# Layer 1's modulation sums placed in the gate and up phase, and more raw slabs in flight in the context's down pass

## The chip, the cores and the metric

The kernel runs on one core of a Trainium2 chip. The metric is the device time of one execution in microseconds (us), and the median of several runs counts. Five engines work side by side, each on its own instructions in a fixed order: TensorE (PE, matrix products), VectorE (DVE, element-wise work), ScalarE (ACT, activations and copies), GpSimd (POOL) and SyncE (SP), which here issues nearly all transfers between HBM and the on-chip memory, one after the other from a single queue.

## The reference, cut to what matters

The model has two layers over 1024 latent tokens (`x`) and 256 context tokens (`ctx`), 1024 channels wide. Each layer scales and shifts its normed input by modulation vectors, sends it through three token mixers and an output projection, and then through a gated feed-forward block of 2816 hidden channels:

```python
for l in range(2):
    mod = silu_c @ w_ada[l] + b_ada[l]              # six vectors of 1024: the modulation
    sh_a, sc_a, g_a, sh_f, sc_f, g_f = split(mod)
    mc = split(silu_cc @ w_ada[l][:, :n_c] + ...)    # the same for the context; 2 vectors in layer 1
    hx = rmsnorm(x) * (1 + sc_a) + sh_a
    ...                                              # Fourier mixing, attention, gated recurrence
    x = x + g_a * (concat(fx, ax, rx) @ w_out[l])
    x = x + g_f * swiglu(rmsnorm(x) * (1 + sc_f) + sh_f, w_gate[l], w_up[l], w_down[l])
    if l == 0:                                       # the context takes the same path in layer 0 only
        ctx = ctx + mc[2] * (concat(fc, ac, rc) @ w_out[l])
        ctx = ctx + mc[5] * swiglu(rmsnorm(ctx) * (1 + mc[4]) + mc[3], ...)
return rmsnorm(x, final_norm)
# swiglu(h) = (silu(h @ w_gate) * (h @ w_up)) @ w_down, all of it in float32
```

## The kernel before

**Exact products out of rounded ones.** Each float32 operand is split into a rounded high part and the rest. `split` (line 123) makes the high part on ACT (line 124, a cast) and the low part on DVE (line 125, a subtraction). `mm3` (line 127) then issues three matmuls: high weight by high activation (L131), high weight by low activation (L132) and low weight by high activation (L133). In tile names `hw` and `lw` are the parts of weights, `mh` and `ml` (or `a`, `T`) those of activations. Weights come from HBM as float32 into raw slots (tag `raw`, RAWB=2 of them) and are split into pairs of slots (tags `wh` and `wl`, WB=4 each). So a raw slot is free again when DVE has done its subtraction, and a pair when PE has used it.

**Tokens in three chunks.** Chunk 0 is the context (256 columns), chunks 1 and 2 are the latent tokens (512 columns each). In layer 0 all three are computed, in layer 1 the feed-forward part has only the latent tokens.

**The operand stage (`operands`, line 1041).** Between the output projection (blocks `oacc`, called as `block(d, ci)`) and the first gate product, the residual rows are normed and modulated. `norm(ci)` adds squares over channels with a ones matmul (`ss`, L403) and takes the root. `rows` modulates one block of 128 channels, and `put` splits it into an operand pair. The latent chunks are multiplied by a fast scheme for 2 by 2 blocks, with seven products named "11", "21", "T1", "T2", "22", "T3" and "T4"; sums and differences of the operand rows (`T`, lines 1092 to 1112) are formed first. The differences for "T3" run on POOL (L1105).

**Gate and up (`fast_product` line 1142, `ffn` line 1243).** For each of 11 column groups g, the gate weight and then the up weight go through the seven products: 84 matmuls of 512 columns, and in layer 0 another 48 of 256 columns for the context (`fpc`). DVE mixes weights (`wm`, L1162), makes their low parts, and combines the products (L1188). The gated result leaves for HBM (`da`, L1136).

**The down passes (`down_pass` line 1251, `down_next` line 1290).** In layer 0 the chunks are taken in the order 1, 2, 0, each with the whole of `w_down`: the results of gate and up are read back (`ar`, L1260) and split into `a`; then for each pair (or four) of output blocks, slabs of 128x512 weights are loaded (`rwd`, L421 in `slab`), split and multiplied into `fd`. A pass has 48 slabs. After each slab, `step` is called once.

**What `step` does.** In chunks 1 and 2 it advances layer 1's modulation sums (`ada_sums`, line 248) by one piece. These read the whole of layer 1's `w_ada` in 96 loads of 128x512 (`wa`, 256 KB each, WAB=2 slots), each multiplied by a scalar per partition and added into a sum `as` on DVE (L278, or L280 for the first of a group; 128 operations in all). A group of four sums (tag `acc`, ACB=4 slots) is then reduced over partitions by ones matmuls (`adas`, L286), copied (`adar`), transposed (`adat`, L301) and put into `mod`. In chunk 0, `step` instead modulates the new rows of chunks 1 and 2 for layer 1's mixers (L324 to L331, with half of the low parts on POOL, L328).

**Who sets the order.** The program is written once in Python; a scheduler with a timing model of its own orders each engine's instructions when the program is built. On the chip each engine keeps that order and waits on semaphores. SP holds the transfers of all these stages in one order too, so a transfer that waits for its slot holds up those behind it.

Of the kernel before, what the change touches and what calls it, by code (L numbers as in the profile page):

```python
# [10 lines left out]
F32 = mybir.dt.float32  # L11
# [72 lines left out]
ACB = 4  # L84
# [15 lines left out]
class Kern:  # L100
# [147 lines left out]
    def ada_sums(self, l, blocks, tags):  # L248
# [5 lines left out]
        groups = [blocks[i:i + 4] for i in range(0, len(blocks), 4)]  # L254
# [39 lines left out]
    def ada_columns(self, l, ps, group):  # L294
# [3 lines left out]
        nc.scalar.copy(out=rowsb, in_=ps)  # L298
        pt = self.ps("pv", f"adat{l}")
        for b in range(4):  # L300
            nc.tensor.transpose(pt[:, b * P:(b + 1) * P], rowsb[:, b * P:(b + 1) * P], self.c["ident"])  # L301
# [115 lines left out]
    def slab(self, src, name, halves=False):  # L417

        nk = src.shape[1]
        raw = self.wp.tile([P, nk, P], F32, tag="raw", name="r" + name, bufs=RAWB)  # L420
# [145 lines left out]
    def unit_prepare(self, l, i, j, ci, ops):  # L566
# [38 lines left out]
        mh = self.sp.tile([8, 2, P], F32R, tag="mh", name="mh", bufs=2)  # L605
# [434 lines left out]
    def operands(self, l, slab, block, ss):  # L1040
# [21 lines left out]
        for d in range(4, KD):  # L1062
            slab(d)
            if l == 0:
                block(d, 0)
            block(d, 1)
        slab(4)
        if l == 0:
            rc = self.rstd(self.square_sum(ss[0], 0), CTX, D, f"f{l}rc", "pa", PAB)
        norm(1)  # L1070
        u = []
        for d in range(4, KD):
# [3 lines left out]
            for e in (2 * d - 8, 2 * d - 7):  # L1076
                u.append(rows(e, 1))
                put(("11", "21")[e // 4], u[e], self.hh[e][:, c1], self.hl[e][:, c1])
                if l == 0:
                    self.modulate(self.xT[e][:, 0:CTX], rc[:, :CTX], e, 1, l, 4, 3, self.hh[e][:, 0:CTX], self.hl[e][:, 0:CTX])  # L1080
        puts = self.puts(0)
        self.fp = itertools.cycle(("mm", "sc", "mx", "pv"))
        first = [self.fast_product(l, w, 0, *tb, put, True) for w, tb, put in zip(("w_gate", "w_up"), (("pa", PAB), ("t2", TB)), puts)]
        next(first[0])
        norm(2)
# [15 lines left out]
        for k in range(4):  # L1101
            put("22", v[4 + k], self.hh[4 + k][:, c2], self.hl[4 + k][:, c2])
# [37 lines left out]
    def fast_product(self, l, w, g, tag, bufs, put, early=False):  # L1140
# [53 lines left out]
        c = context_block()  # L1194
        context(c, a, 0, True)
# [3 lines left out]
        context(c, a, 1, False)  # L1199
# [10 lines left out]
        if l == 0:  # L1210
            put(0, 0, c)
# [24 lines left out]
        if l == 0:  # L1236
            c = context_block()
            context(c, a, 1, True)
            context(c, operand(A[1][0]), 0, False)
            put(1, 0, c)  # L1240

    def ffn(self, l):
        for g in range(1, NFF // 2):
            gate, up = self.puts(g)
            for _ in self.fast_product(l, "w_gate", g, "pa", PAB, gate):
                pass
            for _ in self.fast_product(l, "w_up", g, "t2", TB, up):
                pass
# [3 lines left out]
    def down_pass(self, l, ci, groups, tags, take, step=lambda: None):  # L1252
# [4 lines left out]
        rooms = []  # L1257
        for f in range(NFF):
# [262 lines left out]
```

## Time and profile before

| | before |
|---|---|
| median of 3 runs | 3312.84 us (3311.32 to 3314.97) |
| the profiled execution | 3315.27 us |
| its span in the trace | 3313.5 us |
| mean granted TensorE clock | 0.98 of full speed |
| PE busy | 3170.5 us, 96% |
| DVE busy | 1977.4 us, 60% |
| ACT busy | 1394.4 us, 42% |
| POOL busy | 104.5 us, 3% |
| read from HBM | 282.00 MB |

Busy time of PE is modelled: a matmul's end is worked out, so PE can look busy while its matmuls follow each other at less than full speed. The distance between the starts of consecutive matmuls tells more. The program falls into stages one after the other: layer 0's mixers and output projection (to about 900 us), its operand stage (about 875 to 976), gate and up (to 1476), the down passes for chunks 1, 2 and 0 (1476 to 1879), then layer 1's mixers (to about 2600), its operand stage, gate and up (to 3046) and its two down passes (to 3301).

### The profile page before, as it was taken

What the parts mean: (1) busy time and instruction counts of PE and PEld (TensorE: products, weight loads), DVE (VectorE), ACT (ScalarE), POOL (GpSimd) and SP (SyncE); (2) the same over time, 40 slices, a digit from 0 to 9 for tenths busy, and PEclk for the clock granted to TensorE, in tenths of its full rate; (3) what the DMA queues carried; (4) which work ended last, traced back from release to release, by engine and by line L of the source; (5) the groups of instructions that cost most, each with busy time, mean ns of one, the idle gap of its engine ahead of it and who ended that gap; (6) DMA issues with size and microseconds to landing.
All of it is one profiled execution on the core that took longest, in us unless ns stands there. A gap on an engine that the chain in (4) does not pass through costs nothing.

```text
span 3313.5 us, 44692 instructions
## 1 busy us (share of the span) xinstructions
PE 3170.5 (96%) x16810; PEld 2335.8 (70%) x16810; DVE 1977.4 (60%) x3463; ACT 1394.4 (42%) x2526; POOL 104.5 (3%) x77
## 2 busy tenths in 40 slices
PE   7999999999989999998997899999999899999998
PEld 4977544456868888886776788645556578887887
DVE  5298767552575555566756336677633766667343
ACT  5255455453442322333424334454463533334343
POOL 1000000000110000000001000000000100000000
PEclk9999999999999999998998999999999899999999
DMA  8346110035312122147875432201034222224453
GB/s 275 114 147 218 40 64 29 20 94 176 101 52 71 62 75 71 63 155 230 253 211 172 123 123 81 90 19 62 27 96 159 73 84 85 89 81 159 149 172 95
DMA packets 358657, 369.50 MB, mean 112 GB/s; under 512 B 21896, under 2 KB 268072, under 8 KB 358440
## 3 DMA queue, kind: packets, MB, share of 16 engines
q1 hardware_dynamic: 358440, 366.65, 35.2%
q8 instruction: 131, 2.15, 0.3%
q14 instruction: 86, 0.70, 0.1%
HBM read 282.00 MB, written 84.41 MB: 111 GB/s over the span
## 4 chain that ended last, share of the span: by engine, by line
PE 79%; DMA 8%; DVE 7%; ACT 3%; issue 2%; POOL 0%; SPq 0%; ACTq 0%; DVEq 0%; POOLq 0%
PE fp L131 8%; PE fp L132 8%; PE fp L133 8%; PE pv L639 6%; PE fd L133 3%; PE fd L131 3%; PE fd L132 3%; PE mx L596 3%; DMA rwd<-in_w_down_dram 3%; PE sm L644 3%; PE sc L630 3%; PE u L131 3%; PE u L132 3%; PE u L133 3%; PE sc L631 2%; DMA wa<-in_w_ada_dram 2%
## 5 line engine op out<-in xcount | busy, mean ns | idle before, releaser
L131 PE MATMUL fd<-a,hwd 128*128 128x512 f32 (+1 forms) x880 | 338.0, 384 | 34.3 <-ACT hwd L124 34.3
L133 PE MATMUL fd<-a,lwd 128*128 128x512 f32 (+1 forms) x880 | 337.6, 384 | 17.6 <-DVE lwd L125 17.3
L132 PE MATMUL fd<-a,hwd 128*128 128x512 f32 (+1 forms) x880 | 333.9, 379 | 0.1
L597 DVE TENSOR_REDUCE mp<-mx 128x1 f32<-128x512 f32 (+1 forms) x400 | 223.9, 591 | 131.4 <-PE mx L596 129.9
L125 DVE TENSOR_TENSOR lwd<-rwd,hwd 128x512 fp32r<-128x512 f32 (+1 forms) x240 | 157.3, 657 | 223.2 <-ACT hwd L124 207.6
L124 ACT CAST hwd<-rwd 128x512 fp32r<-128x512 f32 (+1 forms) x240 | 140.1, 584 | 354.6 <-DMA rwd<-in_w_down_dram 196.8
L633 ACT ACTIVATE p<-sc 128x512 f32<-128x512 f32 (+1 forms) x336 | 185.9, 586 | 185.6 <-PE sc L631 182.8
L639 PE MATMUL pv<-p,V 128*64 128x512 f32 (+1 forms) x672 | 230.6, 607 | 0.0
L131 PEld LDWEIGHTS fd<-a,hwd 128*128 128x128 f32 x880 | 174.0, 198 | 70.8 <-ACT hwd L124 40.6
L133 PEld LDWEIGHTS fd<-a,lwd 128*128 128x128 f32 x880 | 173.8, 198 | 55.5 <-DVE lwd L125 27.7
L132 PEld LDWEIGHTS fd<-a,hwd 128*128 128x128 f32 x880 | 173.9, 198 | 30.2 <-issue 1.9
L278 DVE SCALAR_TENSOR_TENSOR as<-wa,sc,as 128x512 f32<-128x512 f32 x224 | 161.2, 748 | 47.4 <-DMA wa<-in_w_ada_dram 46.5
L131 PE MATMUL fp<-mh,hw_gate 128*128 128x512 f32 x352 | 140.3, 399 | 7.7 <-ACT hw_gate L124 4.0
L133 PE MATMUL fp<-mh,lw_gate 128*128 128x512 f32 x352 | 139.5, 396 | 4.4 <-DVE lw_gate L125 4.4
L132 PE MATMUL fp<-ml,hw_gate 128*128 128x512 f32 x352 | 140.0, 398 | 1.6 <-DVE ml L1059 1.5
L131 PE MATMUL fp<-mh,hw_up 128*128 128x512 f32 x352 | 138.4, 393 | 0.2 <-ACT hw_up L124 0.2
L132 PE MATMUL fp<-ml,hw_up 128*128 128x512 f32 x352 | 137.5, 391 | 0.0
L133 PE MATMUL fp<-mh,lw_up 128*128 128x512 f32 x352 | 137.2, 390 | 0.1
L131 PE MATMUL u<-a0hh,hwin 128*128 128x512 f32 (+1 forms) x360 | 133.2, 372 | 3.4 <-ACT a0hh L330 2.1
L132 PE MATMUL u<-a0hl,hwin 128*128 128x512 f32 (+1 forms) x360 | 129.6, 362 | 3.9 <-POOL a0hl L328 2.4
L131 PE MATMUL oacc<-mh,hwo 128*128 128x512 f32 (+1 forms) x320 | 122.2, 384 | 9.8 <-ACT mh L124 8.4
L133 PE MATMUL u<-a0hh,lwin 128*128 128x512 f32 (+1 forms) x360 | 127.8, 356 | 0.0
(356 smaller groups left out, 7398.7 us busy)
## 6 DMA issues: line engine op xcount, KB each, us to landing
rwd<-in_w_down_dram SPq DMA_DIRECT2D x200, 256.0 KB
wa<-in_w_ada_dram SPq DMA_DIRECT2D x192, 256.0 KB
rw_gate<-in_w_gate_dram SPq DMA_DIRECT2D x44, 512.0 KB
rw_up<-in_w_up_dram SPq DMA_DIRECT2D x44, 512.0 KB
da<-mw_gate SPq DMA_DIRECT2D x88, 256.0 KB
ar<-da SPq DMA_DIRECT2D x88, 256.0 KB
rwin<-in_w_in_dram SPq DMA_DIRECT2D x30, 512.0 KB
rwo<-in_w_out_dram SPq DMA_DIRECT2D x24, 512.0 KB
```

The costliest lines, as they stand in the source:

```text
L124: self.nc.scalar.copy(out=hi, in_=src)
L125: self.nc.vector.tensor_tensor(out=lo, in0=src, in1=hi, op=ALU.subtract)
L131: self.nc.tensor.matmul(out, lh, rh, start=(first and i == 0), stop=False)
L132: self.nc.tensor.matmul(out, lh, rl, start=False, stop=False)
L133: self.nc.tensor.matmul(out, ll, rh, start=False, stop=(last and i == n - 1))
L278: nc.vector.scalar_tensor_tensor(out=acc, in0=w, scalar=sc, in1=acc, op0=ALU.mult, op1=ALU.add)
L596: nc.tensor.matmul(mx[:, :kn], Q1[a][:, t * P:(t + 1) * P], self.K1[g][:, k0:k0 + kn])
L597: nc.vector.tensor_reduce(out=mp[:, a * nt + t, i:i + 1], in_=mx[:, :kn], axis=AX.X, op=ALU.max)
L630: nc.tensor.matmul(sc[:, :n], self.K1[g][:, ks], Q1[a], start=True, stop=False)
L633: nc.scalar.activation(out=pf, in_=sc[:, :n], func=AF.Exp, scale=0.125)
L639: nc.tensor.matmul(pv[64 * a:64 * a + 64, :n], self.V[:, i, 64 * g:64 * g + 64], ps[i][a], start=(i == 0), stop=(i == nk - 1))
L644: nc.tensor.matmul(sm[r:r + 32, :n], self.c["first"], ps[i - 1 + o][a], start=(i == 1), stop=(i == nk - 1), tile_position=(0, r))
```

## The change

1. Layer 1's sums move from the steps of the down passes for chunks 1 and 2 into `ffn`: each of the five yields of every gate and up product for g = 1 to 10 advances them by one piece; what is left is issued ahead of the down passes. They are taken in eight groups of two sums instead of four groups of four. `ada_columns` copies and transposes only the rows that are used.
2. In the context's down pass the raw slabs cycle through one slot of tag `raw` and two of tag `acc`; ACB is 5 instead of 4, so that 2 + 5 raw slabs can be in flight. In the other passes the raw slabs use the two raw slots as before.
3. In the operand stage, `norm(2)` is issued ahead of the first products. In layer 0 two of the context's output blocks, (6, 0) and (7, 0), follow it, and the context's norm and modulation come after the operands of "T4". The first products of gate and up (g = 0) do their context part at their end; for this two more weight blocks per product are split again.
4. The low parts of operand "22" are subtracted on POOL instead of DVE, in both layers.
5. The slots for the softmax's row maxima (`mh`) go from two to one.

```diff
-ACB = 4
+ACB = 5
...
-    def ada_sums(self, l, blocks, tags):
+    def ada_sums(self, l, blocks, tags, size=4):
...
-        groups = [blocks[i:i + 4] for i in range(0, len(blocks), 4)]
+        groups = [blocks[i:i + size] for i in range(0, len(blocks), size)]
...
-        nc.scalar.copy(out=rowsb, in_=ps)
+        n = 32 * (max(r for r, g in group) // 32 + 1)
+        nc.scalar.copy(out=rowsb[0:n], in_=ps[0:n])
...
-            nc.tensor.transpose(pt[:, b * P:(b + 1) * P], rowsb[:, b * P:(b + 1) * P], self.c["ident"])
+            nc.tensor.transpose(pt[:, b * P:b * P + n], rowsb[0:n, b * P:(b + 1) * P], self.c["ident"][0:n, 0:n])
...
-        raw = self.wp.tile([P, nk, P], F32, tag="raw", name="r" + name, bufs=RAWB)
+        raw = (self.wp if tag[0] == "raw" else self.tp).tile([P, nk, P], F32, tag=tag[0], name="r" + name, bufs=tag[1])
...
-        mh = self.sp.tile([8, 2, P], F32R, tag="mh", name="mh", bufs=2)
+        mh = self.sp.tile([8, 2, P], F32R, tag="mh", name="mh", bufs=1)
...
-            if l == 0:
+            if l == 0 and d < KD - 2:
                 block(d, 0)
...
-        if l == 0:
-            rc = self.rstd(self.square_sum(ss[0], 0), CTX, D, f"f{l}rc", "pa", PAB)
         norm(1)
...
-                if l == 0:
-                    self.modulate(self.xT[e][:, 0:CTX], rc[:, :CTX], e, 1, l, 4, 3, self.hh[e][:, 0:CTX], self.hl[e][:, 0:CTX])
...
+        norm(2)
+        if l == 0:
+            block(KD - 2, 0)
+            block(KD - 1, 0)
         next(first[0])
-        norm(2)
         next(first[1])
...
-            put("22", v[4 + k], self.hh[4 + k][:, c2], self.hl[4 + k][:, c2])
+            put("22", v[4 + k], self.hh[4 + k][:, c2], self.hl[4 + k][:, c2], nc.gpsimd)
...
+        if l == 0:
+            r = self.rstd(self.square_sum(ss[0], 0), CTX, D, f"f{l}rc", "pa", PAB)
+            self.modulate_chunk(l, 4, 3, 0, r)
...
-        c = context_block()
-        context(c, a, 0, True)
+        if not early:
+            c = context_block()
+            context(c, a, 0, True)
...
+            if early:
+                e = context_block()
+                context(e, operand(A[0][0]), 0, True)
+                context(e, operand(A[0][1]), 1, False)
+                put(0, 0, e)
             put(1, 0, c)
 
     def ffn(self, l):
+        bg = iter(())
+        if l + 1 < DEPTH:
+            bg = self.ada_sums(l + 1, [(b, s) for b in range(4) for s in range(2)] + [(b, 0) for b in range(4, 12)], ("wa",) * WAB, 2)
         for g in range(1, NFF // 2):
             gate, up = self.puts(g)
...
+            for args in ("w_gate", g, "pa", PAB, gate), ("w_up", g, "t2", TB, up):
+                for _ in self.fast_product(l, *args):
+                    next(bg, None)
+        for _ in bg:
+            pass
...
+        raws = itertools.cycle((("raw", RAWB),) if ci else (("raw", RAWB), ("acc", ACB), ("acc", ACB)))
...
-                if ci:
-                    next(bg, None)
-                elif todo:
+                if todo:
                     todo.pop(0)()
...
-                for _ in bg:
-                    pass
```

What moves in the order of the engines is seen at three places.

First, DVE near the start of layer 0's gate product for g = 1. Names end in a running number; `wm` is a mixed weight block, `lw_gate1` the low part of a weight block, `mw_gate` a combination of products, `as1` a modulation sum and `wa1` its load. Before:

```order
L1162 TENSOR_TENSOR wm_8850<-rw_gate1_0_8783,rw_gate1_1_8785 128x512
L125 TENSOR_TENSOR lw_gate1_8821<-rw_gate1_1_8785,hw_gate1_8820 128x512
L1135 TENSOR_TENSOR gc_8457<-fpc_8752,gc_8457 128x256
L125 TENSOR_TENSOR lw_gate1_8853<-wm_8850,hw_gate1_8852 128x512
L1162 TENSOR_TENSOR wm_8875<-wm_8850,rw_gate1_0_8783 128x512
L1162 TENSOR_TENSOR wm_8895<-rw_gate1_1_8785,wm_8875 128x512
L1162 TENSOR_TENSOR wm_8917<-rw_gate1_0_8783 128x512
L125 TENSOR_TENSOR lw_gate1_8878<-wm_8875,hw_gate1_8877 128x512
```

And after:

```order
L1165 TENSOR_TENSOR wm_8900<-wm_8866,rw_gate1_0_8799 128x512
L278 SCALAR_TENSOR_TENSOR as1_8875<-wa1_1_0_8877,sc32_149,as1_8875 128x512
L278 SCALAR_TENSOR_TENSOR as1_8876<-wa1_1_0_8877,sc32_149,as1_8876 128x512
L125 TENSOR_TENSOR lw_gate1_8903<-wm_8900,hw_gate1_8902 128x512
L1165 TENSOR_TENSOR wm_8924<-rw_gate1_1_8801,wm_8900 128x512
L278 SCALAR_TENSOR_TENSOR as1_8875<-wa1_2_0_8906,sc32_149,as1_8875 128x512
L278 SCALAR_TENSOR_TENSOR as1_8876<-wa1_2_0_8906,sc32_149,as1_8876 128x512
L125 TENSOR_TENSOR lw_gate1_8928<-wm_8924,hw_gate1_8927 128x512
L1165 TENSOR_TENSOR wm_8950<-rw_gate1_0_8799 128x512
L278 SCALAR_TENSOR_TENSOR as1_8875<-wa1_3_0_8931,sc32_149,as1_8875 128x512
L278 SCALAR_TENSOR_TENSOR as1_8876<-wa1_3_0_8931,sc32_149,as1_8876 128x512
```

Two operations of a sum now stand between one low part of a weight and the next. In the gate products of g = 1 to 4 sixteen of them stand together in this way (eight loads, two operations each), in the up products of these groups none; from g = 5 on the groups have sixteen loads with one operation each.

Second, SP at the start of the context's down pass (`rwd0_00_4` is the slab of chunk 0, output block 0, from row 4 of the hidden blocks; `xa`, `dx` and `xo` are rows of the residual stream). Before:

```order
L421 DMA rwd0_00_0_15429<-in_w_down_dram 128x4x128
L264 DMA wa1_7_10_15290<-in_w_ada_dram 128x512
L421 DMA rwd0_01_0_15451<-in_w_down_dram 128x4x128
L264 DMA wa1_7_11_15293<-in_w_ada_dram 128x512
L1318 DMA xa_15469<-dx1_0_103 128x512
L421 DMA rwd0_00_4_15475<-in_w_down_dram 128x4x128
L1318 DMA xa_15516<-dx1_1_104 128x512
L421 DMA rwd0_01_4_15498<-in_w_down_dram 128x4x128
```

And after, with the five slabs that SP has issued far ahead, in the middle of the pass for chunk 1 (`rwd0_11_12` is a slab of that pass), and then the first at the start of the context's own pass:

```order
L422 DMA rwd0_01_0_15499<-in_w_down_dram 128x4x128
...
L422 DMA rwd0_00_4_15523<-in_w_down_dram 128x4x128
L422 DMA rwd0_11_12_13732<-in_w_down_dram 128x4x128
L422 DMA rwd0_00_8_15571<-in_w_down_dram 128x4x128
L422 DMA rwd0_01_8_15593<-in_w_down_dram 128x4x128
L422 DMA rwd0_01_12_15640<-in_w_down_dram 128x4x128
...
L422 DMA rwd0_00_0_15477<-in_w_down_dram 128x4x128
L422 DMA rwd0_01_4_15546<-in_w_down_dram 128x4x128
L422 DMA rwd0_00_12_15617<-in_w_down_dram 128x4x128
L422 DMA rwd0_00_16_15665<-in_w_down_dram 128x4x128
```

The loads of `w_ada` are gone from between the slabs. At the start of the first down pass (chunk 1), all 22 loads of `ar` and the last group's loads of `w_ada` now stand ahead of the fourth slab, `rwd0_13_0`; before, sixteen of the `ar` stood between it and the fifth, `rwd0_10_4`.

Third, PE around the sum of squares of chunk 2 in layer 0 (`ss2`; `oacc` is a block of the output projection, `fp` and `fpc` products of gate and up). Before:

```order
L132 MATMUL fpc_8291<-ml0_7_7239,hw_gate0_8304 128x256
L133 MATMUL fpc_8291<-mh0_7_7231,lw_gate0_8305 128x256
L403 MATMUL ss2_8334<-sqa2_7242,ones_152 128x512
L131 MATMUL fp_8349<-mh0_0_7224,hw_up0_8345 128x512
L132 MATMUL fp_8349<-ml0_0_7232,hw_up0_8345 128x512
```

And after:

```order
L133 MATMUL oacc_8171<-mh0_0_7224,lwo0_6_0_8035 128x256
L131 MATMUL oacc_8171<-mh0_1_7225,hwo0_6_0_8034 128x256
L404 MATMUL ss2_8166<-sqa2_7242,ones_152 128x512
L132 MATMUL oacc_8171<-ml0_1_7233,hwo0_6_0_8034 128x256
L133 MATMUL oacc_8171<-mh0_1_7225,lwo0_6_0_8035 128x256
```

The sum of squares now comes within the context's output blocks, ahead of the products "11" and "21" of both gate and up (48 matmuls of 512 columns), where before it came after the gate's.

## Rows read from the trace of the kernel before

**Rows 1.** Section 1 of the page: busy time, share of the span, instructions.

```profile
PE 3170.5 (96%) x16810; PEld 2335.8 (70%) x16810; DVE 1977.4 (60%) x3463; ACT 1394.4 (42%) x2526; POOL 104.5 (3%) x77
```

**Rows 2.** Windows in layer 0's gate and up: length, engines' busy time, PEclk, DMA share, GB/s.

```profile
1100.00:1150.00 50.00, 50.00 (x267) 43.28 (x266) 27.69 (x45) 15.07 (x26) 0.00 (x0) 1.00 0.22 69
1450.00:1475.00 25.00, 25.00 (x135) 21.67 (x134) 18.33 (x31) 8.45 (x14) 0.00 (x0) 1.00 0.51 158
```

**Rows 3.** Groups by line, down passes of chunks 1 and 2 (1476 to 1759 us).

```profile
L131 PE MATMUL fd<-a,hwd 128*128 128x512 f32 x352 | 142.3, 404 | 14.5 <-ACT hwd L124 14.5
...
L278 DVE SCALAR_TENSOR_TENSOR as<-wa,sc,as 128x512 f32<-128x512 f32 x103 | 74.8, 749 | 31.8 <-DMA wa<-in_w_ada_dram 31.3
```

**Rows 4.** Waits of the engines in the same stretch: total us, times, longest.

```profile
ACT hwd L124 <- DMA rwd<-in_w_down_dram: 100.2, 56, 5.6
...
DVE as L278 <- DMA wa<-in_w_ada_dram: 31.3, 33, 2.3
```

**Rows 5.** Timelines at the down passes' bounds (PE; SP's reads of ar): start, duration.

```profile
1475.96 0.40 PE L131 MATMUL fd<-a,hwd 128*128 128x512 f32 x1
...
1479.31 13.54 SPq L1260 DMA_DIRECT2D ar<-da  x16
...
1497.78 0.80 PE L131 MATMUL fd<-a,hwd 128*128 128x512 f32 x1 [10.25 <-ACT hwd L124]
...
1757.81 0.40 PE L133 MATMUL fd<-a,lwd 128*128 128x512 f32 x1
...
1878.05 0.28 PE L133 MATMUL fd<-a,lwd 128*128 128x256 f32 x1
...
3046.07 0.39 PE L131 MATMUL fd<-a,hwd 128*128 128x512 f32 x1
...
3299.42 0.39 PE L133 MATMUL fd<-a,lwd 128*128 128x512 f32 x1
...
3300.78 0.39 PE L133 MATMUL fd<-a,lwd 128*128 128x512 f32 x1
```

**Rows 6.** Windows in the context's down pass, and that of chunks 1 and 2.

```profile
1476.00:1759.00 283.00, 259.52 (x1096) 204.49 (x1094) 187.80 (x314) 97.82 (x177) 0.00 (x0) 0.96 0.77 236
...
1775.00:1800.00 25.00, 16.45 (x100) 14.88 (x100) 25.00 (x30) 15.89 (x28) 10.92 (x7) 0.85 0.53 156
...
1850.00:1875.00 25.00, 19.84 (x125) 18.01 (x124) 8.97 (x15) 6.93 (x12) 0.00 (x0) 0.86 0.43 125
```

**Rows 7.** Waits in the context's down pass (1759 to 1880 us).

```profile
ACT hwd L124 <- DMA rwd<-in_w_down_dram: 54.0, 29, 3.9
...
PE fd L131 <- ACT hwd L124: 14.0, 12, 2.3
```

**Rows 8.** Groups by line and shape in the context's down pass.

```profile
L125 DVE TENSOR_TENSOR lwd<-rwd,hwd 128x512 fp32r<-128x512 f32 x40 | 30.3, 760 | 42.6 <-ACT hwd L124 39.5 <-PE fd L133 1.5 <-PE fd L132 1.4
...
L324 DVE SCALAR_TENSOR_TENSOR hf<-xo,mod,sqa 128x512 f32<-128x512 f32 x8 | 9.0, 1130 | 0.6 <-ACT sqa L1329 0.6
L324 DVE SCALAR_TENSOR_TENSOR hf<-xa,mod,sqa 128x512 f32<-128x512 f32 x8 | 7.0, 871 | 0.0
L331 DVE SCALAR_TENSOR_TENSOR a1hl<-hf,mod,a1hh 128x512 fp32r<-128x512 f32 x8 | 6.7, 869 | 0.0
```

**Rows 9.** PE timeline at a group's ones matmuls, and all transposes (min/median/max ns).

```profile
1538.32 1.06 PE L286 MATMUL adas<-as,ones 128*32 128x512 f32 x8
...
L301 PE MATMUL adat<-c_ident,adar x36: 270/272/333, 53.1 to 1773.4; 128*128 128x128 f32 x36
```

**Rows 10.** Layer 0's operand stage: a window, then DVE and POOL timelines.

```profile
925.00:950.00 25.00, 16.84 (x49) 9.93 (x50) 21.02 (x34) 12.62 (x24) 14.27 (x4) 0.80 0.00 1
...
939.11 0.68 DVE L1059 TENSOR_TENSOR ml<-xT,mh 128x512 fp32r<-128x512 f32 x1
...
942.65 1.77 DVE L1188 TENSOR_TENSOR mw_gate<-mw_gate 128x512 f32<-128x512 f32 x1
...
933.88 9.99 POOL L1105 TENSOR_TENSOR xT<-xT,xT 128x512 f32<-128x512 f32 x3 [4.60 <-ACT xT L1054]
```

More of the change, by code (lines that the diff above doesn't have):

```diff
@@ L415, in piece, with slab @@
         return [self.wp.tile([P, nk, P], F32R, tag=tag, name=tag[1] + name, bufs=WB) for tag in ("wh", "wl")]
-    def slab(self, src, name, halves=False):
+    def slab(self, src, name, halves=False, tag=("raw", RAWB)):
         nk = src.shape[1]
-        raw = self.wp.tile([P, nk, P], F32, tag="raw", name="r" + name, bufs=RAWB)
+        raw = (self.wp if tag[0] == "raw" else self.tp).tile([P, nk, P], F32, tag=tag[0], name="r" + name, bufs=tag[1])
         self.nc.sync.dma_start(out=raw, in_=src)
@@ L1198, in fast_product @@
         plus(z, p, x)
-        context(c, a, 1, False)
+        if not early:
+            context(c, a, 1, False)
         if early:
@@ L1209, in fast_product @@
         put(0, 1, z)
-        if l == 0:
+        if l == 0 and not early:
             put(0, 0, c)
@@ L1239, in fast_product @@
             context(c, operand(A[1][0]), 0, False)
+            if early:
[3 more added lines that the diff above has]
+                put(0, 0, e)
             put(1, 0, c)
     def ffn(self, l):
+        bg = iter(())
+        if l + 1 < DEPTH:
+            bg = self.ada_sums(l + 1, [(b, s) for b in range(4) for s in range(2)] + [(b, 0) for b in range(4, 12)], ("wa",) * WAB, 2)
         for g in range(1, NFF // 2):
             gate, up = self.puts(g)
-            for _ in self.fast_product(l, "w_gate", g, "pa", PAB, gate):
-                pass
-            for _ in self.fast_product(l, "w_up", g, "t2", TB, up):
-                pass
+            for args in ("w_gate", g, "pa", PAB, gate), ("w_up", g, "t2", TB, up):
[3 more added lines that the diff above has]
+            pass
         self.load = self.exp_ln_set(self.last_silu)
@@ L1270, in down_pass @@
                 for d, acc in zip(ds, accs):
-                    hi, lo = self.slab(self.I["w_down"][l, P * f0:P * (f0 + m), d * P:(d + 1) * P].rearrange("(k p) c -> p k c", p=P), f"wd{l}_{ci}{d}_{f0}")
+                    hi, lo = self.slab(self.I["w_down"][l, P * f0:P * (f0 + m), d * P:(d + 1) * P].rearrange("(k p) c -> p k c", p=P), f"wd{l}_{ci}{d}_{f0}", tag=next(raws))
                     self.mm3(acc, [(hi[k], lo[k], *a[f0 + k]) for k in range(m)], f0 == 0, f0 + m == NFF)
@@ L1292, in down_next @@
         nc = self.nc
-        bg = self.ada_sums(l + 1, [(b, s) for b in range(4) for s in range(2)] + [(b, 0) for b in range(4, 12)], ("wa",) * WAB)
         tags = itertools.cycle(("mx", "sc", "mm"))
@@ L1331, in down_next @@
             if ci == 2:
-                for _ in bg:
-                    pass
                 self.new_h(f"a{l + 1}")
```

## The prediction

> **What bounds the kernel now.** I read first the busy shares [rows 1]. PE is busy for 3170.5 of 3313.5 us, DVE for 60%. A busy PE is a modelled figure, so the second view is the start times of matmuls where a stage begins and ends, against the spacing that the same shape has when nothing disturbs it. Six spacings of 512-column matmuls at the end of the last pass take 3300.78 − 3299.42 = 1.36 us, or 0.227 us each [rows 5]. In gate and up, 267 matmuls start in 50 us [rows 2], so a product of 84 wide and 48 narrow ones takes 132 × 50 / 267 = 24.7 us; the wide ones are 84 × 0.227 = 19.0 of it, and the narrow ones (24.7 − 19.0) / 48 = 0.118 us each. Three stages can be measured against this.
>
> Layer 0's gate and up run without a gap at full clock, with DVE busy for 27.7 of 50 us [rows 2]: bound by PE, with room on DVE. Layer 0's down passes for chunks 1 and 2 take from 1475.96 to 1757.81 and the last 0.4, 282.2 us for 1056 wide matmuls [rows 5] that need 1056 × 0.227 = 239.4; 43 us are lost. Layer 1's two passes have the same 1056 matmuls without any sums, and take 3046.07 to 3300.78, 254.7 us [rows 5]. The context's pass takes the 120 us from there to 1878.05 [rows 5] for 528 narrow matmuls, which need 528 × 0.118 = 62.3: some 57 us are lost. The third view, the waits, says to what: the casts of slabs wait for their loads, 100.2 us in chunks 1 and 2 [rows 4] and 54.0 us in the context's pass [rows 7], where PE in turn waits for the casts. With two raw slots a load can only start when DVE has done with the slab two before it, so the time from issue to landing is paid over and over, while the transfer engines are at 0.43 of their time and 125 GB/s, against 0.77 and 236 GB/s in chunks 1 and 2 [rows 6]. PE's granted clock falls too, to 0.85 and 0.86 in windows with such gaps [rows 6].
>
> **Part 1, the sums.** Out of the down passes go DVE work (103 of the operations at 749 ns are there, 74.8 us, [rows 3]), DVE's waits for their loads (31.3 us, [rows 4]), and 25 MB of transfers from SP's queue, each of which holds the slabs behind it until DVE frees its slot. What is left is like layer 1's two passes, 254.7 us. One thing differs: the start. Before, PE ran out of slabs at the start and waited 10.25 us, until 1497.78, while SP issued sixteen reads of ar for 13.5 us ahead of the fifth slab [rows 5]. Afterwards all reads of ar and the last `wa` loads stand ahead of even the fourth. PE then has three slabs of 12 matmuls, 36 × 0.227 = 8.2 us, until about 1484, and the fourth still lands at about 1496: a stall of about 12 us. The sum: 239.4, the stall of 12, and what layer 1's passes lose beyond theirs, which I put at 8 us of their 15.3, give 259 against 282.2, **−23 us**. The ends: 250 (−32) if the stall goes, and 269 (−13) if the last sixteen loads, 4.2 MB, which at 236 GB/s [rows 6] are 18 us, push the slabs back by half of that.
>
> Into gate and up go 128 operations of 749 ns at the most, 96 us over ten groups of 49 us each. DVE has about 22 of 50 us free there [rows 2], 220 us in all, so they fit on average. This has even been seen: the window 1450 to 1475 holds the first of these sums, with DVE at 18.3 of 25 us and PE still at 25.00 and full clock [rows 2]. Not hidden is PE's own part: the ones matmuls of a group take 1.06 us, however many sums it has [rows 9], and four transposes of at most 0.27 us each [rows 9] another 1; eight groups give 8 × 1.06 + 8 × 0.35 (they overlap) to 8 × 2.1, 11 to 17 us, of which I take 11. The four groups that this takes out of the down passes are already in the 259. For g = 1 to 4 sixteen operations stand in one gate product. DVE then has 13.9 + 16 × 0.75 = 25.9 us for a product of 24.7, plus the waits for loads, 31.3 / 33 = 0.95 us each as in the down passes [rows 4], 8 × 0.95 = 7.6. That is 33.5 us, 8.8 too many; the up product behind it, with no sums, gives 10.9 back. The weights split ahead and in the raw slots cover about 6 to 8 us of this, and I let 1 us in all reach PE. **+12 us**; ends +9 (loads issued so early that nothing waits) and +40 (three quarters of 8.8 us reach PE in four products).
>
> **Part 2, seven raw slabs.** The context's pass becomes limited by PE or DVE instead of by landing times. Five slabs are issued during the pass for chunk 1, so the start has cover. PE needs 62.3 us. But in the first sixteen slabs DVE also modulates 16 rows for layer 1: its groups of 9.0, 7.0 and 6.7 us beside 16 × 0.76 for the low parts [rows 8] make 34.9 us, in which PE has 16 × 11 × 0.118 = 20.8 us to do. In the window 1775 to 1800 DVE was full, 25.00 of 25 [rows 6]; this stays. So 62.3 + 34.9 − 20.8 = 76.4, and with a wait at the change of passes **about 79 us instead of 120, −41**. The ends: −52, if the modulation is spread over more slabs, and −28, if PE's clock stays at 0.85 in all of the pass (76 / 0.85 = 90, and the wait).
>
> **Part 3, the operand stages.** In layer 0 the sum of squares of chunk 2 comes some 15 us earlier, and PE has the "11" and "21" products of both weights behind it. In 925 to 950 PE was busy for 16.8 of 25 us at clock 0.80, with DVE at 21.0 and POOL at 14.3 [rows 10]: DVE is what is late there, and it still has all the operands to make. The change removes four subtractions per layer from it (0.68 us each, [rows 10]) and moves the context's modulation behind "T4", where PE has work; it adds four weight splits. I take −2 us in layer 0 and −1 in layer 1, with ends −10 and +8 together. Against it speaks POOL: while it ran three subtractions in 9.99 us, one DVE operation took 1.77 us instead of about 0.68 [rows 10]. Four more such meetings cost DVE 4 × 1.1 = 4.4 us, where 4 × 0.6 = 2.4 us were saved; that is in the upper end.
>
> The Trainium skill, in SBUF — State Buffer, section "SBUF: two separate sides", says of this that DVE and GpSimd share one pair of ports by an exclusive lock, held for a whole instruction, when a DVE operation has two inputs in SBUF. By that rule moving "22" between the two saves DVE nothing, and part 3 would come to about +1 instead of −3, and the median to 3262 us. The 1.77 us agrees with it, though the 0.68 us of another operation during the same POOL stretch shows that not every one is stopped [rows 10].
>
> The second slot for `mh` and the smaller copies of the sums count nothing: the units that use `mh` follow each other much more slowly than a slot is held, and the copy is off PE's path; if that cover is gone, it is a microsecond or two.
>
> **The sum.** −23 + 12 − 41 − 3 = −55. Against the profiled execution's 3315.3 us that is 3260; that execution lies 2.4 us above the median, so the median becomes **3258 us**.
>
> **The rivals.**
> (a) *The sums show through in gate and up, and the clock falls* (slower). If DVE comes late in most of the twenty products, PE has gaps, and gaps of 5 to 9 us in 25 went with a granted clock of 0.85 [rows 6]. The 490 us of g = 1 to 10 at 0.88 would cost 490 × (1 / 0.88 − 1) = 67 us: 3258 + 67 = **3325**. [...] For it: one gate product in five is overfull by my count. Against: the up products have no sums there, and the window at 1450 shows no loss [rows 2].
> (b) *The context's pass keeps its pace* because the cast, low part and matmul of each slab follow one another, or because the loads in SP's single order still wait for each other's slots. Half of the gain remains, −20: **3279**. For it: PE's clock is low there. Against: the casts wait for loads by 54.0 us, by far the most [rows 7].
> (c) *The down pass's start grows*: the last group of sums, the reads of ar and the slabs meet at 1476, and the stall rises from 12 to some 25 us: **3271**.
> (d) *Everything overlaps better*: the ends of parts 1 to 3 on the good side, −32 + 9 − 52 − 8 = −83: **3230**.
>
> **How the numbers follow.** My forecast, within 8 us of 3258, or near it, has 0.50; (a) 0.06, (b) 0.17, (c) 0.15, (d) 0.12. The range reaches from the better half of (d) to beyond (b), **3236 to 3287**, and leaves out (a), the lower part of (d) and a doubled (b). A measurement can tell about 0.2%, 6.6 us. All but (a) are faster by more: faster 0.93, same 0.02, slower 0.05 (part of (a) ends near no change).
>
> **What would show it.** In the profile after: gate and up of layer 0 still near 24.7 us a product, plus 1 to 1.4 us for each of eight groups of ones matmuls and transposes, no PE wait for `lw_gate` above 1 us, DVE at 70 to 80%; the passes for chunks 1 and 2 near 259 us with one stall of about 12 us after the third slab; the context's pass near 79 us, with the casts' wait for `rwd` small, the first sixteen slabs at over 2 us each and the rest at 1.3; the operand stages within a few us. I am wrong if PE waits for low parts in the gate products of g = 1 to 4, or if the context's slabs still take 2 us each at the end of their pass.

## The result and the profile after

The changed kernel takes 3267.96 us in the median (3264.48 to 3269.34), the kernel before 3313.9 us in the same series: a ratio of 0.986, 95% interval 0.984 to 0.988, or some 46 us saved. The forecast was 3258 with a range of 3236 to 3287. The profiled execution took 3264.5 us against the 3315.3 of before, with a span of 3262.7.

The stages, from the starts of their matmuls in the two traces (gate and up of g = 0 belong to the operand stage, which is counted here from the first output-projection block on):

| stage | before, us | after, us | change | predicted |
|---|---|---|---|---|
| layer 0, output projection to g = 1 | 201.3 | 205.5 | +4.3 | −2 |
| layer 0, gate and up, g = 1 to 10 | 497.2 | 509.9 | +12.7 | +12 |
| down passes of chunks 1 and 2 | 283.2 | 260.6 | −22.6 | −23 |
| context's down pass | 119.0 | 76.4 | −42.6 | −41 |
| layer 1's mixers | 623.5 | 620.4 | −3.1 | 0 |
| layer 1, output projection to g = 1 | 163.7 | 164.9 | +1.3 | −1 |
| layer 1, gate and up, g = 1 to 10 | 380.8 | 380.8 | 0.0 | 0 |
| layer 1, down passes | 254.7 | 252.6 | −2.1 | 0 |

Section 1 of the page of after answers to [rows 1]:

```profile
PE 3143.9 (96%) x16826; PEld 2322.2 (71%) x16826; DVE 1983.9 (61%) x3459; ACT 1403.6 (43%) x2538; POOL 109.0 (3%) x85
```

DVE does nearly the same work as before (1977.4 us there); most of the change only puts it elsewhere. The next windows of after answer to [rows 2, 6]: one in gate and up, the down passes of chunks 1 and 2, and the context's pass (length; busy time of PE, PEld, DVE, ACT and POOL; PEclk, DMA share, GB/s).

```profile
1100.00:1150.00 50.00, 50.00 (x266) 42.34 (x265) 35.40 (x56) 15.53 (x27) 0.00 (x0) 1.00 0.32 101
...
1494.00:1755.00 261.00, 246.29 (x1072) 200.58 (x1071) 119.69 (x201) 95.99 (x178) 0.00 (x0) 0.97 0.58 181
...
1755.00:1775.00 20.00, 16.59 (x116) 15.25 (x116) 18.63 (x24) 15.17 (x26) 5.26 (x4) 0.91 0.64 192
1775.00:1795.00 20.00, 16.22 (x116) 15.11 (x115) 19.79 (x27) 13.13 (x24) 7.09 (x5) 0.91 0.68 197
1795.00:1815.00 20.00, 20.00 (x169) 20.00 (x168) 10.56 (x20) 9.66 (x18) 0.00 (x0) 1.00 0.72 213
```

In gate and up DVE has gone from 27.7 to 35.4 of 50 us, 71%, and PE is still never idle, at full clock. The context's pass falls into two halves: for 40 us DVE is nearly full and PE waits for it, and then PE runs through.

The start of the down passes, in PE's timeline of after, answers to [rows 5]:

```profile
1505.42 2.81 PE L286 MATMUL adas<-as,ones 128*32 128x512 f32 x4 [2.78 <-DVE as L278]
1508.90 0.69 PE L302 MATMUL adat<-c_ident,adar 64*128 64x64 f32 x4 [0.67 <-ACT adar L299]
1520.17 0.79 PE L131 MATMUL fd<-a,hwd 128*128 128x512 f32 x1 [10.58 <-ACT hwd L124]
```

The last group of sums is finished here, 11 us into the pass, and then PE waits 10.6 us for a slab. With the two small waits this is 14 us, where 12 were predicted. In the context's pass the waits (total us, times, longest) answer to [rows 7]:

```profile
ACT hwd L124 <- PE fd L132: 23.5, 27, 2.3
...
PE fd L133 <- DVE lwd L125: 7.0, 6, 3.2
```

The casts wait for their slots to be used by PE, and no longer for loads.

### The profile page after: what moved, and what is told of

Its sections match the earlier page's. It is cut to its first block, busy times and chain, and to the rows that moved or that the text cites. A ratio compares the mean times of both kernels' runs of the same rounds, so it can differ in the third digit from the quotient of the medians.

```text
span 3262.7 us, 44741 instructions
## 1 busy us (share of the span) xinstructions
PE 3143.9 (96%) x16826; PEld 2322.2 (71%) x16826; DVE 1983.9 (61%) x3459; ACT 1403.6 (43%) x2538; POOL 109.0 (3%) x85
## 4 chain that ended last, share of the span: by engine, by line
PE 84%; DVE 7%; DMA 4%; ACT 3%; issue 1%; SPq 0%; POOL 0%; DVEq 0%; ACTq 0%; POOLq 0%
PE fp L131 8%; PE fp L133 8%; PE fp L132 8%; PE pv L640 6%; PE fd L131 5%; PE fd L133 5%; PE fd L132 5%; PE mx L597 3%; PE sm L645 3%; PE sc L631 3%; PE u L131 3%; PE u L132 3%; PE u L133 3%; PE sc L632 2%; PE oacc L132 2%; PE oacc L131 2%
## 5 line engine op out<-in xcount | busy, mean ns | idle before, releaser
L131 PE MATMUL fd<-a,hwd 128*128 128x512 f32 (+1 forms) x880 | 327.3, 372 | 14.7 <-ACT hwd L124 14.7
L133 PE MATMUL fd<-a,lwd 128*128 128x512 f32 (+1 forms) x880 | 327.6, 372 | 7.2 <-DVE lwd L125 7.0
L132 PE MATMUL fd<-a,hwd 128*128 128x512 f32 (+1 forms) x880 | 325.5, 370 | 0.0
L131 PEld LDWEIGHTS fd<-a,hwd 128*128 128x128 f32 x880 | 167.9, 191 | 43.0 <-ACT hwd L124 15.3
L132 PEld LDWEIGHTS fd<-a,hwd 128*128 128x128 f32 x880 | 167.9, 191 | 27.7 <-issue 0.2
```

The source lines that it names most:

```text
L131: self.nc.tensor.matmul(out, lh, rh, start=(first and i == 0), stop=False)
L132: self.nc.tensor.matmul(out, lh, rl, start=False, stop=False)
L133: self.nc.tensor.matmul(out, ll, rh, start=False, stop=(last and i == n - 1))
```

## Experiments: the operand stage

The step that failed is the operand stage: some 3 us saved by the prediction, 5.5 us lost in the trace. The clearest sign in after is the time between layer 0's first gate product and g = 1, 77.2 us before and 81.4 after, with a wait of PE in it that the kernel before doesn't have:

```profile
944.53 0.79 PE L131 MATMUL fp<-T,hw_gate 128*128 128x512 f32 x1 [6.27 <-ACT T L1059]
```

ScalarE's timeline of after, around the cast that PE waits for, and below it a line of DVE's, show why:

```profile
937.81 1.28 ACT L315 ACT_TABLE_LOAD   x1
939.11 0.47 ACT L315 ACTIVATE f0rc<-ss,eps 128x256 f32<-128x256 f32 x1
939.60 1.28 ACT L1133 ACT_TABLE_LOAD   x1
940.89 0.63 ACT L1133 ACTIVATE mw_gate<-mw_gate 128x512 f32<-128x512 f32 x1
941.54 1.28 ACT L316 ACT_TABLE_LOAD   x1
942.83 0.42 ACT L316 ACTIVATE f0rc<-f0rc 128x256 f32<-128x256 f32 x1
943.86 0.62 ACT L1059 CAST T<-xT 128x512 fp32r<-128x512 f32 x1 [0.61 <-DVE hf L325]
...
953.19 1.28 ACT L1133 ACT_TABLE_LOAD   x1
...
943.28 0.48 DVE L325 SCALAR_TENSOR_TENSOR hf<-xT,mod,f0rc 128x256 f32<-128x256 f32 x1 [0.98 <-ACT f0rc L316]
```

(The cast that PE waits for is the one at 943.86.) The context's root (Ln at L315, Exp at L316) has moved behind "T4", into the time of the first silus (L1133), and each change between the two kinds of function loads a table for 1.28 us. Three loads stand ahead of the cast; a fourth, for the silu behind the Exp, follows at 953.19. The cast itself waits for `hf`, the first rows of the context's modulation on DVE, and those waited for the Exp. The Trainium skill, ScalarE: Activation LUTs, section "What ACT_TABLE_LOAD costs", gives 1283 ns for the load, which is what the rows show, and some 1380 ns of drain beside it, which these rows don't show: the next activation starts 0.02 us after the load.

The second suspect was POOL. DVE's timeline of after, where PE waited 3.2 and 3.7 us for weights, and POOL's beside it:

```profile
916.31 1.75 DVE L1098 TENSOR_TENSOR T<-xT,T 128x512 f32<-128x512 f32 x1
917.99 1.75 DVE L1165 TENSOR_TENSOR wm<-wm,rw_gate 128x512 f32<-128x512 f32 x1
919.66 1.75 DVE L125 TENSOR_TENSOR lw_gate<-wm,hw_gate 128x512 fp32r<-128x512 f32 x1
921.34 1.76 DVE L1060 TENSOR_TENSOR T<-T,T 128x512 fp32r<-128x512 f32 x1
923.03 1.77 DVE L125 TENSOR_TENSOR lw_gate<-wm,hw_gate 128x512 fp32r<-128x512 f32 x1
...
914.58 4.62 POOL L1105 TENSOR_TENSOR xT<-xT,xT 128x512 f32<-128x512 f32 x3 [11.83 <-ACT xT L1055]
919.16 5.08 POOL L1060 TENSOR_TENSOR ml<-xT,mh 128x512 fp32r<-128x512 f32 x3
```

Six operations of POOL stand in a row, about 1.6 us each, and five of DVE's take 1.75 instead of 0.68 us; with two more at 928 to 932 that is seven.

**The context's root ahead of the first products** (root_early):

```diff
             block(KD - 1, 0)
+            r = self.rstd(self.square_sum(ss[0], 0), CTX, D, f"f{l}rc", "pa", PAB)
         next(first[0])
...
-            r = self.rstd(self.square_sum(ss[0], 0), CTX, D, f"f{l}rc", "pa", PAB)
             self.modulate_chunk(l, 4, 3, 0, r)
```

> The changed kernel, with the context's root (square sum, Ln, Exp) written ahead of the first products again; its modulation stays behind the operands of T4. Measure: layer 0 from the first gate product's first matmul to the start of g = 1, 77.2 us before and 81.4 after. Theory A (the late root: on ScalarE its Ln and Exp stand between two silus, so that three activation tables of 1.28 us are loaded in 5 us, and the first T4 operand waits behind them; PE waits 6.27 us for it): the wait falls to 2 us or less, the stage to about 77 us, the total by 4 us against the changed kernel. Theory B (the low parts of 22 on GpSimd stretch DVE operations from 0.68 to 1.75 us): the stage stays within 1 us of 81.4.

Measured: 3265.97 us, ratio 0.9865 (0.985 to 0.988). The table loads are gone from the place, and the stage takes 77.8 us instead of 81.4, as theory A has it; in the four kernels that keep the changed stage as it is (after, two_raw, drained and ar_between) it takes 80.1 to 82.4. The wait itself fell only to 3.97 us, not to 2, since DVE's modulation of the context still stands ahead of the cast. The total can't show 3.6 us: its interval is ±0.15%, 5 us.

**The low parts of "22" on VectorE** (lo22_dve):

```diff
-            put("22", ..., self.hl[4 + k][:, c2], nc.gpsimd)
+            put("22", ..., self.hl[4 + k][:, c2])
```

> The changed kernel, with the low parts of 22 on VectorE again, in both layers. Theory A (the late root): layer 0's stage of 81.4 us changes by less than 1 us, and PE's 6.27 us wait for the first T4 operand is still there. Theory B (GpSimd holds up DVE: seven DVE operations of about 1.75 us between 916 and 931 us, some 7 us in all, and waits of PE of 3.2 and 3.7 us for weights): layer 0's stage falls by 3 to 5 us, and layer 1's, from its first gate product to g = 1, 70.7 us after and 66.9 before, by 3 to 4 us; the total by 6 to 9 us.

Measured: 3265.61 us, ratio 0.9866 (0.985 to 0.988). Layer 0's stage takes 79.3 us, 2.1 less; layer 1's 68.9, 1.8 less. DVE's stretched operations there are three instead of seven, and PE still waits 5.08 us for the first "T4" operand. Theory B had 3 to 5 and 3 to 4 us, so POOL's part is smaller than that, and two things limit what these differences show. In layer 0 ScalarE's order changed along with the edit: no silu stands between Ln and Exp any more (their loads are at 938.90 and 941.20), so that one load of 1.28 us is gone too. And the same code varies by some 2 us between traces: layer 1's stage takes 70.5 to 72.6 us in the five kernels that have "22" on POOL (72.6 in root_early, which edits nothing there), and 68.0 to 69.7 in the three that have the rest of the new stage but "22" on VectorE. These groups don't overlap, so in layer 1 POOL costs about 2 us; in layer 0 its part isn't separated from the load's.

**Both edits** (root_early_lo22):

> Both of these edits in the changed kernel. If A and B each hold for a part: layer 0's stage at about 74 us, below the 77.2 of before, since the square sum of chunk 2 still comes 16.7 us earlier; layer 1's at 67; the total 8 to 11 us below the changed kernel. If the two losses cover each other: 77, and no more than the better of the single edits.

Measured: 3260.43 us, ratio 0.9853 (0.984 to 0.987); layer 0's stage 77.1, layer 1's 69.7. The two losses cover each other: with the root early, POOL's part is worth only 0.7 us (77.8 to 77.1), and the stage is back at the 77.2 of before, not at 74.

**The whole operand stage of before** (old_operands; the functions `operands` and `fast_product` as they were, all else as changed):

> The changed kernel with the whole operand stage and the first products as before; sums and raw slabs as changed. Theory A and B alike: the stages return to 77.2 and 66.9 us, the total falls by 5 to 8 us against the changed kernel, so that the operand stage's part of the change by itself costs that much. Rival: the stages are slower for another reason (the context blocks between, the moved sums): they stay at 81 and 70.

Measured: 3259.95 us, ratio 0.9847 (0.983 to 0.986); the stages 77.0 and 68.6. That is 8 us below the changed kernel by the medians, 4 by the ratios.

Taken over all traces, the whole of layer 0's part, from the first output-projection block to g = 1, lasts 200.5 to 203.6 us in the six kernels with the old stage and 204.4 to 210.5 in the four with the changed one, 5.6 more on average. Layer 1's lasts 160.5 to 167.2 and 164.9 to 169.2 (five kernels), 3.0 more on average, and these ranges overlap.

What is left open is the part ahead of layer 0's first gate product. From the first output-projection block to it, the kernels with the old stage took 123.5 to 126.4 us, those with the new one 124.2 to 128.2, with granted clocks of 0.66 (both_mended, below) and 0.86 (old_op_ar) in the window 780 to 805 of two of them. The ranges overlap, and the code is nearly the same; whether the new order costs something here isn't settled.

## Experiments: the slabs and the sums

**Two raw slots again in the context's pass** (two_raw):

```diff
-        raws = itertools.cycle((("raw", RAWB),) if ci else (("raw", RAWB), ("acc", ACB), ("acc", ACB)))
+        raws = itertools.cycle((("raw", RAWB),))
```

> The changed kernel, with the context's raw slabs in the two raw slots as before (ACB stays 5). Theory: the slots give the whole gain of the context's pass; it takes 112 to 119 us again instead of 76.3 (118.9 before), the casts wait for slabs by 45 us or more, and the total is 36 to 43 us above the changed kernel. Rival: much of the gain came with the sums' leaving SP's queue and with the clock that no longer falls; then the pass takes about 95 us.

Measured: 3310.63 us, ratio 0.9987 (0.998 to 0.9996). The context's pass takes 112.3 us. Its waits and a window of its second part:

```profile
ACT hwd L124 <- DMA rwd<-in_w_down_dram: 46.1, 26, 4.9
...
1800.00:1872.00 72.00, 57.76 (x371) 50.35 (x369) 25.14 (x43) 20.93 (x38) 0.00 (x0) 0.93 0.39 116
```

Without the slots the rest of the change is worth 0.1%. Here neither DVE nor the transfers are busy, and PE still gets a slab only every 2.1 us: the casts wait for loads that waited for a slot.

**The slots alone** (slots_alone: the kernel before with ACB 5, one slot for `mh`, and the line above as in the changed kernel):

> The kernel before with only the context's raw slabs in seven slots (ACB 5, one slot for mh); the sums stay in chunks 1 and 2, the operand stage as before. Theory: the context's pass falls from 118.9 to 76 to 82 us, chunks 1 and 2 stay at 280 to 284 us, the total falls by 36 to 43 us. Rival: without the sums' leaving, SP's queue holds the early slabs back and the pass takes 95 us or more.

Measured: 3279.3 us, ratio 0.9889 (0.987 to 0.991). Chunks 1 and 2 take 278.9 us. The context's pass takes 85.2: less than the rival's 95, more than the theory's 76 to 82. Where the difference lies is seen when the pass's 528 matmuls are cut into six parts of 88, eight slabs' worth each, in us from the first start to the next part's:

| slabs | 1 to 8 | 9 to 16 | 17 to 24 | 25 to 32 | 33 to 40 | 41 to 48 |
|---|---|---|---|---|---|---|
| before | 26.1 | 25.0 | 15.5 | 17.7 | 17.1 | 17.6 |
| two_raw | 18.7 | 24.9 | 17.7 | 17.0 | 16.8 | 17.2 |
| slots_alone | 23.8 | 18.1 | 11.6 | 10.6 | 10.6 | 10.5 |
| after | 16.1 | 18.1 | 10.5 | 10.6 | 10.5 | 10.6 |

The slots take 4 to 7 us off every eight slabs from the ninth on, and 2 to 3 off the first eight. The sums' leaving takes another 7.4 off the first eight without the slots and 7.7 with them. What ran on DVE around the change of passes, from 1740 to 1840 us, hints at a cause: before, ten operations of the sums (7.4 us, and 5.5 us of waits for their loads) and eleven low parts of ar; after, none of the sums and one of ar. Two_raw has none of the sums and seven of ar there, with nearly the same gain, which speaks for the sums; no run separates the two. The prediction gave the whole of this stage to the slots; a sixth to a fifth of it (6.7 us in two_raw, 8.8 in slots_alone) is the sums'.

**The sums finished within gate and up** (drained):

```diff
-                for _ in self.fast_product(l, *args):
+                for i, _ in enumerate(self.fast_product(l, *args)):
                     next(bg, None)
+                    if i == 2:
+                        next(bg, None)
```

> The changed kernel, with the sums advanced twice at one of the five yields of every product, so that all of them are finished within gate and up. Theory: at the start of the down passes the waits of 2.8 and 0.7 us and the ones matmuls of 2.8 us at low clock go, and gate and up gain one more group of 1.85 us; the wait of 10.6 us behind the reads of ar stays. The total falls by 3 to 5 us. Rival: the denser sums show in gate and up as PE waits of more than 3 us in all, and nothing is gained.

Measured: 3262.38 us, ratio 0.984 (0.9825 to 0.9854). Gate and up take 511.9 us, 2.0 more, without any wait of PE; chunks 1 and 2 take 252.0, 8.6 less. The wait for the slab is still there, 8.99 us. The gain is 6.6 us by the stages, more than expected.

**The reads of ar between the slabs** (ar_between, on top of drained):

```diff
+        def read(upto):
+            for f in range(len(a), min(NFF, upto)):
...                                                   # the loop over ar as it was
+        if ci != 1:
+            read(NFF)
         for ds in groups:
...
                 m = min(4, NFF - f0)
+                read(f0 + 4)
                 for d, acc in zip(ds, accs):
```

> As drained, and in the pass for chunk 1 of each layer the reads of ar are written between the slabs of the first four output blocks, four ahead of each row of slabs, instead of all ahead. Theory (the stall at the start of the down passes is made by sixteen reads of ar ahead of a slab in SP's order): the wait of 10.6 us goes, the two passes take 246 to 250 us instead of 260.6, the total falls by 12 to 15 us against the changed kernel. Rival: the reads of ar themselves are late, and PE waits as long for a low part of ar instead.

Measured: 3245.63 us, ratio 0.9791 (0.978 to 0.9805). A window over the two passes:

```profile
1501.70:1743.20 241.50, 240.57 (x1060) 198.59 (x1060) 113.19 (x188) 93.94 (x174) 0.00 (x0) 1.00 0.58 180
```

The passes take 241.5 us, 2 above the 239.4 that the matmuls need, below the range expected, and layer 1's passes fall to 246.8; by the medians the total is 22 us below the changed kernel. The rival's wait for ar doesn't appear. What made the stall is seen in drained, which still has it, in the lines of SP, ScalarE and PE:

```profile
1497.81 11.95 SPq L1277 DMA_DIRECT2D ar<-da  x13
1509.82 0.98 SPq L422 DMA_DIRECT2D rwd<-in_w_down_dram  x2
...
1514.69 0.62 ACT L124 CAST hwd<-rwd 128x512 fp32r<-128x512 f32 x1 [0.88 <-DMA rwd<-in_w_down_dram]
...
1515.36 0.80 PE L131 MATMUL fd<-a,hwd 128*128 128x512 f32 x1 [8.99 <-ACT hwd L124]
```

Thirteen reads stand ahead of the slab for 12 us, and its cast, once reached, waits for the slab to land. The edit moves the casts and low parts of ar along with the reads, so it doesn't separate SP's order from theirs; but ScalarE's waits in this stretch of drained are all for loads, so the order in SP's queue is what held the slab back: its turn was late.

**The mended operand stage, and the old one, on top of this** (both_mended: the two edits of root_early_lo22; old_op_ar: `operands` and `fast_product` of before):

> ar_between with the operand stage of root_early_lo22 (the early square sum of chunk 2 and the context's two late blocks kept, the context's root early, the low parts of 22 on VectorE). Layer 0's stage at 77 us instead of 82, layer 1's at 69 to 70, the down passes of chunks 1 and 2 at 241.5: total 4 to 8 us below ar_between.

> ar_between with the operand stage and first products of the kernel before. If what is left of the changed operand stage is worth something once it is mended, this is slower than both_mended; if it is worth nothing, the two agree within 3 us: layer 0's stage 77, layer 1's 68 to 70.

Measured: 3238.2 us, ratio 0.9779 (0.976 to 0.9795), and 3235.39 us, ratio 0.9771 (0.976 to 0.9785). Layer 0's stage is 77.1 and 77.0 us, layer 1's 68.0 and 66.7. They agree within 3 us: norming chunk 2 earlier brings nothing that these runs can show, even when its two costs are taken away.

**The modulations spread over the context's pass** (spread, on top of old_op_ar):

```diff
+                count[0] += 1
-                if todo:
+                if todo and count[0] % 3 == 1:
                     todo.pop(0)()
```

> old_op_ar with the sixteen modulations in the context's pass taken at every third slab instead of at each of the first sixteen. Theory (the first sixteen slabs are bound by DVE at 34 us, where PE needs 20.8): the pass falls from 76.4 to 64 to 68 us, with each eight slabs at 10.5 to 11.5 us. Rival: later rows meet the end of the pass and layer 1's start waits for them, so that what the pass gains the mixers lose.

Measured: 3232.41 us, ratio 0.9762 (0.975 to 0.978). The pass takes 73.1 us instead of 76.3, far from 64 to 68; the mixers lose nothing (619.5), so the rival fails too. The eights are 11.6, 13.9, 11.9, 14.6, 10.6 and 10.5: better at first and worse behind. Around a wait of PE of 2.07 us at 1755, DVE's and POOL's timelines:

```profile
1751.82 1.79 DVE L325 SCALAR_TENSOR_TENSOR hf<-xa,mod,sqa 128x512 f32<-128x512 f32 x1
1753.53 0.86 DVE L1291 SCALAR_TENSOR_TENSOR xo<-fd,mod,xo 128x256 f32<-128x256 f32 x2
1754.32 1.28 DVE L125 TENSOR_TENSOR lwd<-rwd,hwd 128x512 fp32r<-128x512 f32 x2
...
1751.59 1.47 POOL L329 TENSOR_TENSOR a1hl<-hf,a1hh 128x512 fp32r<-128x512 f32 x1 [3.57 <-ACT a1hh L328]
```

POOL's eight operations, one for every second modulation, all lie in the first 32 slabs: the scheduler placed the work earlier than at every third slab. Here one operation that POOL stretches stands ahead of two low parts, together with the results of a block. The pass is DVE-bound in places, as the theory has it, but the edit didn't spread the work as far as it was meant to.

**Groups of three** (spread_s3, on top of spread: `("wa",) * WAB, 3` in `ffn`):

> spread with layer 1's sums in groups of three instead of two (six groups instead of eight, 104 loads instead of 96). Theory (a group costs PE 1.85 us however many sums it has, and DVE's part is hidden): gate and up fall from 511.9 to about 508 us, the total by 3 to 4 us. Rival: more loads and fewer free acc slots for the mixed weights make PE wait in gate and up by more than that.

Measured: 3231.1 us, ratio 0.9755 (0.974 to 0.9775). Gate and up fall to 506.3 us, 5.6 less, without a wait of PE, and chunks 1 and 2 rise to 243.1, since the last group now ends there. A group of three costs PE 1.6 us (products of 26.46 to 26.48 us against 24.86), not the 1.85 that was expected. In the total the 1.3 us are within the interval. This kernel and the one ahead of it are the fastest here, some 2.4% below the kernel before.

## Why the prediction was right, and where it was not

*Part 1, the sums.* Right in its mechanism and near in its sizes. DVE's 96 us are hidden, and PE's own part is all that shows: a product that holds a whole group is longer than 24.86 us by 1.8 (26.69 to 26.71), and seven groups by 1494 us give 12.7. The prediction took 1.4 per group and 1 us for DVE coming late; the true figures are 1.8 and 0. That sixteen operations are too many for one gate product was argued from waits of 0.95 us a load. Over gate and up DVE waited 26.0 us in 35 waits for the loads, 0.74 each, and none of it reached PE; that the weights split ahead covered it is likely, but not tested. The chunks' passes came out at 260.6 against 259, with the stall where it was put. The 8 us beyond the stall measured 7.2 (260.6 − 239.4 − 14.0), but they weren't a loss that the passes have anyway, as the prediction took it from layer 1's: without the stall and the group that ends beside it, ar_between loses 2.1. That group's ones matmuls and transposes take 3.5 us, with a granted clock of 0.53 from 1505 to 1521 us and 0.89 in the ten us after. Rival (a) had nothing to start from: the granted clock is 1.00 over all of gate and up. Rival (c) was not seen, though its 3271 lies nearer to the measured time than 3258: the stall is 14 us, not 25.

*Part 2, the slabs.* Right: 76.4 us against 79; the first sixteen slabs took 34.2 us against 34.9 worked out from DVE's rows, and the rest 1.32 us each. Most of the gain in the first eight was credited to the wrong part, as slots_alone shows. Rival (b) fell: the casts wait for PE.

*Part 3, the operand stages.* Wrong in sign: +5.5 us instead of −3. The step that failed is "moves the context's modulation behind T4, where PE has work": with the modulation went its root, and the cost of moving a root among silus, three loads of 1.28 us on ScalarE ahead of the cast and one behind it, stands in no term of the sum; root_early gives it as 3.6 us. The second step, POOL, was named with its price (1.1 us for a meeting, four meetings) and left in the upper end. The traces have just four more stretched DVE operations in each layer, seven against three in lo22_dve, 4.3 us against the 2.4 saved; layer 1's stages put the loss at 2 us, and in layer 0 it shows as 0.7 to 2. DVE still is the fullest engine there, which is the likely reason that the earlier norm gave nothing; no run tests it. The windows of after at the place of [rows 10], and the one ahead of it:

```profile
900.00:925.00 25.00, 18.16 (x83) 14.77 (x83) 24.68 (x31) 17.20 (x30) 10.61 (x7) 0.88 0.18 53
925.00:950.00 25.00, 15.39 (x44) 9.91 (x42) 20.85 (x33) 16.46 (x27) 4.76 (x4) 0.78 0.10 31
```

DVE, the third engine in the row, is busy for 24.68 of the first 25 us, and PE's clock falls with its gaps, to 0.88 and 0.78.

By the rule on the shared ports that the prediction cites, part 3 was to be +1. The measured +5.5 lies nearer to that than to −3, but in part by luck: 3.6 us of it are the root's, which that rule doesn't touch. The Trainium skill says in the same page (SBUF — State Buffer, section "Who interferes with whom") that the order of issue decides who is blocked. These rows fit that, though no run changes the order alone: before, with three POOL operations in 9.99 us, it was mostly POOL that took long [rows 10]; after, with six in 9.7 us, five DVE operations did.

*What was not forecast.* Layer 1's mixers are 3.1 us shorter. That comes with the slots: they take 623.5 us in both kernels with two raw slots (before and two_raw) and 619.1 to 620.4 in the others. Part of it is likely PE's clock, which no longer is low when the context's pass ends (0.93 in the 25 us behind it in before and two_raw, 1.00 in after and slots_alone): 25 us at 0.93 cost 1.8. Layer 1's down passes are 2.1 us shorter, which is within what they vary between runs (252.6 to 254.7 with the same code).

The sum of the parts was −55 and the profiled execution moved by −50.8. Part 3 alone is 8.5 us off, and the 5.2 us that no part had put down make up for more than half of that, so the sum's closeness is partly luck. The median moved by 46: it lies 3.5 us above the profiled execution here, while it was taken to lie 2.4 below, as it did before. That is where most of the difference between 3258 and 3268 comes from.

## What to carry to other kernels

When a stage waits for loads while the transfer engines are half idle, count the raw slots first: with two, each slab pays the whole way from a freed slot to landed data. Background sums hide well under a stage that PE bounds; count only what they put on PE, and let them end inside it. Before a norm is moved, look at what function ScalarE has loaded at the new place, and in one in-order queue look at whose turn a late transfer was waiting for: to write the reads between the slabs gave 17 us (3262.4 to 3245.6), and moving the sums, cost and gain together, 10 us (−22.6 + 12.7) and some 7 more at the start of the context's pass.

## What the hardware showed beyond that

A POOL subtraction of 128x512 takes about 1.6 us in after, and beside it one DVE operation with two inputs on chip takes 1.75 instead of 0.68 us: 1.07 us per meeting, whether it makes T, wm or lw_gate. Eight POOL operations stretch seven of DVE's, four stretch three (lo22_dve). In before, where three POOL operations took 9.99 us [rows 10], only one of DVE's was stretched. The ones matmuls of a group of two sums, and of one sum alone at the end of spread_s3, hold PE as long as those of a group of four, 1.05 against 1.06 us [rows 9]. PE ran through 509 us of gate and up at full clock with 0.00 us of waits while DVE was at 70% and SP's queue waited for DVE's sums 72 times.
